# Attention scores and maxima as 64-row products, with one head of a pair in each half of the rows

## The chip, the core and the metric

The kernel runs on one core of a Trainium2 chip. The core has a matrix engine (TensorE, PE in the rows; its loads of the stationary operand are PEld), VectorE (DVE), ScalarE (ACT), GpSimd (POOL) and SyncE (SP), which here only issues DMAs. Products are written to PSUM, which has 8 banks of 128 partitions by 512 fp32 values. The metric is the device time of one launch in microseconds (us); the time before is the median of three runs.

## What is computed

Two layers of a diffusion backbone over 2048 latent tokens behind 256 context tokens, width 1024. Layer 0 is multi-head latent attention, layer 1 is gated linear attention. Only layer 0's attention is touched. Cut to that:

```python
q = concat(q_nope, axial_rope(q_rope))       # 16 heads, 64 + 32 columns each
k = concat(k_nope, broadcast(axial_rope(kr)))  # kr: 32 columns, the same for all heads
s = einsum('qhd,khd->hqk', q, k) * 96 ** -0.5  # latents read all 2304 tokens, context its own 256
o = einsum('hqk,khe->qhe', softmax(s), v)
y = (o * silu(gate)) @ w_out
```

The kernel computes `exp(s - max)` with the row maximum inside the product, and divides by the sum at the end. Each fp32 operand of a score product is split into a rounded high part and the rest (h and l, both of type F32R), and a score is the sum of three products, kh·qh + kh·ql + kl·qh. Maxima come from kh·qh alone.

## The kernel before

After the projections, attention runs over 8 pairs of heads, and in each pair over 5 chunks of queries: one of 256 context tokens and four of 512. One pair and chunk is a step (40 in all). A step goes over its keys in tiles of 128: 2 for the context chunk, 18 for the others. Step and key tile together are an item, 592 in all, of which 576 are 512 queries wide and 16 are 256 wide.

For one item `scores` (L578) makes a tile `st` of two PSUM banks, one bank for each head `j`, with three products a head (L592 to L594). The stationary operand is 128 keys, the moving one 512 queries, and the contraction is over 96 rows (64 of the head's own, 32 of the rotary part). The first product has a 97th row: ones in the key tile, and minus the row maximum in the query tile. ScalarE then takes the exponential of both banks (L596), and VectorE or GpSimd adds it to a running sum (L601, L603). `values` (L608) follows two items behind, for three key tiles at a time: it multiplies with v (L616), one head in the left 64 columns of the array and one in the right 64, in plain fp32. `finish` (L621) sums over partitions (L628) and normalises.

`maxima` (L460) runs ahead of the scores as a generator. For each step it makes, for a head, 128 queries and up to 512 keys, one product of 96 rows (L475) into a tile `pmx` and a VectorE maximum over it (L476): 40 of them in a full step, of which 8 are 256 wide, and 4 in a context step, 1312 in all. The pool of `pmx` has 3 banks; `st` has 4 and `po` 1. When a step's maxima are there they are transposed (L481), negated (L483) and sent by DMA into row 96 of the query tile (L485). The generator is stepped by a counter: in the query projections (`feed`, L511) up to a lead of 72, then 41 times a full step, spread evenly over the items (L690 to L708).

Keys are in four tiles `kb{b}{s}`, for even and odd pairs, high and low. `key_rows` (L413) puts the shared rotary rows into each of them, for both heads; `load_k` (L421) and `load_q` (L435) load a chunk by DMA, and GpSimd makes its high and low parts (L48, L53 by the helper `K`). All DMAs of these loads are issued by SyncE in the order of the program. The rest of the order of instructions on an engine is made by a scheduler when the program is built, from the order of the source, the dependences and the pools' buffers; so two engines' instructions may stand in another order than the source has them.

Of the kernel before, what the change touches and what calls it, by code (L numbers as in the profile page):

```python
# [19 lines left out]
P = 128  # L20
# [97 lines left out]
def body(ctx, tc, I, out, stop=99, dbg=None):  # L118
# [39 lines left out]
    qr_d = [dram.tile([2, 2, P, n], F32, name=f"qr{c0}_d") for c0, n in CHUNKS]  # L158
# [252 lines left out]
    kb = [[kvp.tile([97, 2, T], F32R, name=f"kb{b}{s}") for s in "hl"] for b in range(2)]  # L411

    def key_rows(b):  # L413
        for s in range(2):
            tc.keep_in_program_order(nc.sync.dma_start(kb[b][s][64:96, :, :].bitcast(F32), kr_d[s].unsqueeze(1).to_broadcast([32, 2, T])))
        tc.keep_in_program_order(nc.sync.dma_start(kb[b][0][96:97, :, :].rearrange("p j t -> p (j t)").bitcast(F32), onesr.bitcast(F32)))
# [4 lines left out]
    def load_k(pr, ci):  # L421

        c0, n = CHUNKS[ci]
        qf = qsp.tile([96, 2, 512], F32, name="kf", tag="qf", bufs=2)
        nc.sync.dma_start(qf[0:64, :, :n], k_d[ci][pr].rearrange("(h d) t -> d h t", h=2))

        def put():
            dst = [kb[pr % 2][s][0:64, :, c0:c0 + n] for s in range(2)]
            i_ = k.hi("p", dst[0], qf[0:64, :, :n])
            if pr == 0 and ci < 2:  # L430
                tc.keep_in_program_order(i_)
            k.lo("p", dst[1], qf[0:64, :, :n], dst[0])
        return put

    def load_q(si):  # L435
        pr, ci = steps[si]
        c0, n = CHUNKS[ci]
        qf = qsp.tile([96, 2, 512], F32, name="qf", tag="qf", bufs=2)
        nc.sync.dma_start(qf[0:64, :, :n], qn_d[ci][pr].rearrange("(h d) t -> d h t", h=2))
        for r in range(2):  # L440
            nc.sync.dma_start(qf[64 + 16 * r:80 + 16 * r, :, :n], qr_d[ci][pr // 4, r, 32 * (pr % 4):32 * (pr % 4) + 32, :].rearrange("(h d) t -> d h t", h=2))

        def put():
            qs = qsp.tile([97, 2, 2, 512], F32R, name="qs", tag="qs")
            k.hi("p", qs[0:96, 0, :, :n], qf[:, :, :n])
            k.lo("p", qs[0:96, 1, :, :n], qf[:, :, :n], qs[0:96, 0, :, :n])
# [13 lines left out]
    def maxima():  # L460

        for si, (pr, ci) in enumerate(steps):
# [7 lines left out]
            for j in range(2):  # L470
                for t in range(nq):
                    for b in range(npart):
                        w = min(512, keys - b * 512)
                        ps = pmp.tile([P, 512], F32, name="pmx")
# [1000 lines left out]
```

## Time and profile before

| | us |
|---|---|
| median of three runs (3830.13 to 3837.49) | 3831.97 |
| the profiled execution, its own time | 3830.01 |
| its span, first to last instruction | 3828.1 |
| the attention stage in it, first score product to last | 671.6 to 2450 |
| VectorE busy in 672 to 2450 | 1277.1 |
| mean granted TensorE clock, share of full speed | 0.985 |

A matmul's duration in the rows is longer than the distance to the next one, because products are pipelined and the profile models their ends. So what a product costs in a stream is read here from the starts of the rows, not from their durations. The rows read "start, duration" and merge neighbours of one kind; the count stands behind the x. An fp32 product (L616) is recorded as two matmuls, an F32R product (L475, L594) as one. A few matmul records can be missing.

### The profile page before, as it was taken

The numbers are of one execution on the slowest core, as the hardware profiler recorded it, in microseconds if no ns is written. First come the engines' busy times: TensorE is split into PE (matmuls) and PEld (weight loads), VectorE is DVE, ScalarE is ACT, GpSimd is POOL, SyncE is SP. The second block draws the span as 40 slices with busy tenths as digits, with TensorE's granted clock in tenths as the row PEclk, the third lists the DMA queues.
The fourth block names the chain that finished last, engine by engine and source line by source line (L and its number), as shares of the span: only waits on it lengthen the run. The fifth ranks groups of instructions, "written<-read, shape, count | busy, mean of one in ns | idle before, by whom it ended". The sixth has DMA issues, their size and how long they took to land.

```text
span 3828.1 us, 51918 instructions
## 1 busy us (share of the span) xinstructions
PE 3702.5 (97%) x20446; PEld 2717.6 (71%) x20446; DVE 2406.3 (63%) x3300; ACT 1356.5 (35%) x1991; POOL 1194.7 (31%) x731
## 2 busy tenths in 40 slices
PE   7999999999999999999999999999999999999799
PEld 5777887655555555555555655687999898999677
DVE  4332436777677777777777776465255677776863
ACT  2332221333333333333333333332224444443431
POOL 3121124646354363634546343455000101000000
PEclk8999999999999999999999999999999999999899
DMA  6120564302120121201101010276775666669332
GB/s 226 67 82 38 182 213 159 91 19 73 43 63 23 37 73 38 65 24 53 32 19 51 17 39 12 67 247 210 264 253 173 223 220 212 229 199 319 135 133 98
DMA packets 277245, 451.43 MB, mean 118 GB/s; under 512 B 21877, under 2 KB 178101, under 8 KB 264969
## 3 DMA queue, kind: packets, MB, share of 16 engines
q1 hardware_dynamic: 212504, 371.09, 29.5%
q10 hardware_dynamic: 64496, 77.02, 5.8%
q8 instruction: 161, 2.64, 0.3%
q14 instruction: 84, 0.68, 0.1%
HBM read 307.14 MB, written 140.71 MB: 117 GB/s over the span
## 4 chain that ended last, share of the span: by engine, by line
PE 76%; DMA 7%; DVE 6%; issue 6%; POOL 3%; ACT 2%; SPq 1%; POOLq 0%; ACTq 0%; DVEq 0%
PE st L594 20%; PE po L616 14%; PE pmx L475 8%; PE pj L61 5%; PE pj L60 5%; PE pj L62 5%; PE pp L893 2%; PE pp L894 2%; PE pp L895 2%; DMA wsg<-in_gla_w_in 2%; PE py L893 1%; PE py L895 1%; PE py L894 1%; PE pk L1060 1%; PE py L62 1%
## 5 line engine op out<-in xcount | busy, mean ns | idle before, releaser
L476 DVE TENSOR_REDUCE mx<-pmx 128x1 f32<-128x512 f32 (+1 forms) x1312 | 762.4, 624 | 320.5 <-PE pmx L475 319.8
L596 ACT ACTIVATE pe<-st 128x1024 f32<-128x1024 f32 (+1 forms) x592 | 599.3, 1013 | 1006.1 <-PE st L594 980.1
L603 POOL TENSOR_TENSOR acc<-acc,pe 128x1024 f32<-128x1024 f32 x192 | 468.5, 2440 | 571.1 <-ACT pe L596 570.4
L616 PE MATMUL po<-pe,vt 128*64 128x512 f32 (+1 forms) x2368 | 571.6, 598 | 0.0
L603 DVE TENSOR_TENSOR acc<-acc,pe 128x1024 f32<-128x1024 f32 x256 | 438.7, 1714 | 97.0 <-ACT pe L596 97.0
L594 PE MATMUL st<-qs,kb0h 97*128 97x512 f32 (+3 forms) x1184 | 375.7, 397 | 0.1
L594 PE MATMUL st<-qs,kb1h 97*128 97x512 f32 (+3 forms) x1184 | 374.9, 397 | 0.0
L616 PEld LDWEIGHTS po<-pe,vt 128*64 128x64 f32 x2368 | 156.7, 137 | 300.5 <-issue 297.1
L893 PE MATMUL pp<-w,ht 128*128 128x256 f32 x1088 | 317.9, 292 | 0.0
L894 PE MATMUL pp<-w,ht 128*128 128x256 f32 x1088 | 305.9, 281 | 0.0
L895 PE MATMUL pp<-w,ht 128*128 128x256 f32 x1088 | 304.9, 280 | 0.0
L594 PEld LDWEIGHTS st<-qs,kb1h 97*128 97x128 f32 (+1 forms) x1184 | 218.5, 190 | 57.4 <-issue 12.2
L594 PEld LDWEIGHTS st<-qs,kb0h 97*128 97x128 f32 (+1 forms) x1184 | 219.9, 190 | 49.1 <-issue 4.2
L594 PE MATMUL st<-qs,kb0l 96*128 96x512 f32 (+1 forms) x592 | 232.4, 393 | 0.0
L594 PE MATMUL st<-qs,kb1l 96*128 96x512 f32 (+1 forms) x592 | 232.1, 392 | 0.0
L1242 POOL TENSOR_TENSOR orr<-oss,mhalf 128x4 f32<-128x4 f32 x16 | 17.1, 1068 | 659.3 <-DVE oss L1241 659.3
L475 PE MATMUL pmx<-kb0h,qs 96*128 96x512 f32 (+1 forms) x656 | 209.0, 397 | 9.0 <-DVE mx L476 5.6
L475 PE MATMUL pmx<-kb1h,qs 96*128 96x512 f32 (+1 forms) x656 | 205.0, 396 | 4.1 <-DVE mx L476 4.0
L893 PEld LDWEIGHTS pp<-w,ht 128*128 128x128 f32 x1088 | 205.8, 189 | 3.4
L894 PEld LDWEIGHTS pp<-w,ht 128*128 128x128 f32 x1088 | 205.9, 189 | 1.1
L895 PEld LDWEIGHTS pp<-w,ht 128*128 128x128 f32 x1088 | 205.5, 189 | 0.1
L475 PEld LDWEIGHTS pmx<-kb1h,qs 96*128 96x128 f32 x656 | 114.0, 189 | 120.9 <-issue 73.7
(398 smaller groups left out, 7311.4 us busy)
## 6 DMA issues: line engine op xcount, KB each, us to landing
ht<-hh_d SPq DMA_DIRECT2D x44, 1024.0 KB
ht<-hl_d SPq DMA_DIRECT2D x44, 1024.0 KB
xt<-in_x SPq DMA_DIRECT2D x32, 512.0 KB
mod_w<-in_ada_w SPq DMA_DIRECT2D x16, 1024.0 KB
v<-gv_d SPq DMA_DIRECT2D x32, 512.0 KB
wsg<-in_gla_w_in SPq DMA_DIRECT2D x66, 192.0 KB
v_d<-vs ACTq DMA_DIRECT2D x18, 512.0 KB
vt<-v_d SPq DMA_DIRECT2D x8, 1152.0 KB
```

The source lines that it names most:

```text
L60: nc.tensor.matmul(ps, ah, bh, start=(i == 0), stop=False)
L61: nc.tensor.matmul(ps, ah, bl, start=False, stop=False)
L62: nc.tensor.matmul(ps, al, bh, start=False, stop=(i == n - 1))
L475: nc.tensor.matmul(ps[:, :w], qs[0:96, 0, j, t * P:t * P + P], kh[0:96, j, b * 512:b * 512 + w], start=True, stop=True)
L476: nc.vector.reduce_max(mx[:, j * nq + t, b:b + 1], ps[:, :w], axis=AX.X)
L594: nc.tensor.matmul(st[:, j, :n], a, b, start=(i == 0), stop=(i == 2))
L596: nc.scalar.activation(pe[:, :, :n], st[:, :, :n], AF.Exp, scale=SCALE)
L603: eng.tensor_tensor(acc[:, :, :n], acc[:, :, :n], pe[:, :, :n], op=ALU.add)
L616: nc.tensor.matmul(po[64 * j:64 * j + 64, :n], vt[:, kt, 64 * j:64 * j + 64], pe[:, j, :n], start=(kt == 0), stop=(kt == nk - 1))
L893: nc.tensor.matmul(ps, ah, bh, start=(i == 0), stop=False)
L894: nc.tensor.matmul(ps, ah, bl, start=False, stop=False)
L895: nc.tensor.matmul(ps, al, bh, start=False, stop=(i == n - 1))
```

## The change

The two heads of a pair are laid in the two halves of the 128 rows: head 0 in rows 0 to 63, head 1 in rows 64 to 127. Keys are now two tiles, `kbs0` and `kbs1` (even and odd pairs), each with a high and a low part of `T` = 2304 columns; `kbs1` also holds two tiles `kr` for all pairs. In each half `kr[0]` has the 32 rotary rows' high part and below it their low part; `kr[1]` has the high part and below it a row of ones. The query tile has the head's own 64 rows in one plane, and in a second plane the 32 rotary rows twice. The low plane's second copy gives its first row to minus the maximum.

A score is five products a head of 64 rows (the last of 33): kh·qh, kh·ql, kl·qh, `kr[0]` with the high rotary rows (both its parts at once), `kr[1]` with the low ones and the maximum. A maximum is two: kh·qh and `kr[0]` with the high rotary rows. The source writes them alternating between the heads, so that neighbours lie in different halves of the rows and in different banks. A unit of `maxima` is now one pair of tiles, both heads; its counters are halved (lead 36, 21 units a full step), and the number of tiles is the same.

```diff
+    kbs = [kvp.tile([P, 8 * D], F32R, name="kbs0"), kvp.tile([P, 4 * T], F32R, name="kbs1")]
+    kb = [[kbs[b][:, s * T:s * T + T] for s in range(2)] for b in range(2)]
+    kr = [kbs[1][:, s * T:s * T + T] for s in (2, 3)]
+    def key_rows():
+        for j in range(2):
+            for i, r0, s in ((0, 0, 0), (0, 32, 1), (1, 0, 0)):
+                tc.keep_in_program_order(nc.sync.dma_start(kr[i][64 * j + r0:64 * j + r0 + 32, :].bitcast(F32), kr_d[s]))
+            tc.keep_in_program_order(nc.sync.dma_start(kr[1][64 * j + 32:64 * j + 33, :].bitcast(F32), onesr[:, 0:T // P].bitcast(F32)))
...
-        for r in range(2):
-            nc.sync.dma_start(qf[64 + 16 * r:80 + 16 * r, :, :n], qr_d[ci][pr // 4, r, 32 * (pr % 4):32 * (pr % 4) + 32, :].rearrange("(h d) t -> d h t", h=2))
+        nc.sync.dma_start(qf[:, 0, :n], qn_d[ci][pr])
+        for j in range(2):
+            for u in range(2):
+                nc.sync.dma_start(qf[64 * j + 32 * u:64 * j + 32 * u + 32, 1, :n], qr_d[ci][pr, j])
...
-                        ps = pmp.tile([P, 512], F32, name="pmx")
-                        nc.tensor.matmul(ps[:, :w], qs[0:96, 0, j, t * P:t * P + P], kh[0:96, j, b * 512:b * 512 + w], start=True, stop=True)
-                        nc.vector.reduce_max(mx[:, j * nq + t, b:b + 1], ps[:, :w], axis=AX.X)
-                        yield
+                    ps = [pmp.tile([P, 512], F32, name="pmx") for _ in range(2)]
+                    for i, kk in enumerate((kh, kr[0])):
+                        for j in range(2):
+                            js = slice(64 * j, 64 * j + 64)
+                            nc.tensor.matmul(ps[j][:, :w], qs[js, 0, i, t * P:t * P + P], kk[js, bs], start=(i == 0), stop=(i == 1))
+                    for j in range(2):
+                        nc.vector.reduce_max(mx[:, j * nq + t, b:b + 1], ps[j][:, :w], axis=AX.X)
+                    yield
...
-    fed, lead, due = 0, 72, 0.0
+    fed, lead, due = 0, 36, 0.0
...
-            for j in range(2):
-                k3 = [(kh[0:97, j, ks], qs[0:97, 0, j, :n]), (kh[0:96, j, ks], qs[0:96, 1, j, :n]), (kl[0:96, j, ks], qs[0:96, 0, j, :n])]
-                for i, (a, b) in enumerate(k3):
-                    nc.tensor.matmul(st[:, j, :n], a, b, start=(i == 0), stop=(i == 2))
+            terms = [(kh, 0, 0, 64), (kh, 1, 0, 64), (kl, 0, 0, 64), (kr[0], 0, 1, 64), (kr[1], 1, 1, 33)]
+            for i, (a, s, r, m) in enumerate(terms):
+                for j in range(2):
+                    js = slice(64 * j, 64 * j + m)
+                    nc.tensor.matmul(st[:, j, :n], a[js, ks], qs[js, s, r, :n], start=(i == 0), stop=(i == len(terms) - 1))
...
-        total = sum(41 if ci else 5 for _, ci in steps)
+        total = sum(21 if ci else 3 for _, ci in steps)
```

Left out: the DRAM layout of the rotary queries, the chunk loads of the keys (one tile of 128 rows where it was 64 rows by two heads), and the output weights, which take over the same two key tiles.

On TensorE, in the sixth pair's third chunk of 512, from one group of value products to the next, the order before is this (`st` is a score tile, `pmx` a tile for maxima, `po` the output):

```order
L616 MATMUL po<-pe,vt 64x512 x6
L475 MATMUL pmx<-kb0h,qs 128x512 x3
L594 MATMUL st<-qs,kb1h 128x512 x2
L594 MATMUL st<-qs,kb1l 128x512
L594 MATMUL st<-qs,kb1h 128x512 x2
L594 MATMUL st<-qs,kb1l 128x512
L475 MATMUL pmx<-kb0h,qs 128x512
L475 MATMUL pmx<-kb0h,qs 128x256
L594 MATMUL st<-qs,kb1h 128x512 x2
L594 MATMUL st<-qs,kb1l 128x512
L594 MATMUL st<-qs,kb1h 128x512 x2
L594 MATMUL st<-qs,kb1l 128x512
```

Between two score groups of six products there stand two or three products for maxima, each in a bank of its own.

At the same place on TensorE the changed program has these rows (`kbs_3830` is the tile of even pairs, `kbs_3831` that of odd pairs and of the rotary rows):

```order
L625 MATMUL po<-pe,vt 64x512 x6
L484 MATMUL pmx<-kbs_3830,qs 128x256 x2
L484 MATMUL pmx<-kbs_3831,qs 128x256 x2
L603 MATMUL st<-qs,kbs_3831 128x512 x10
L484 MATMUL pmx<-kbs_3830,qs 128x512 x2
L484 MATMUL pmx<-kbs_3831,qs 128x512 x2
L603 MATMUL st<-qs,kbs_3831 128x512 x10
L484 MATMUL pmx<-kbs_3830,qs 128x512 x2
L484 MATMUL pmx<-kbs_3831,qs 128x512 x2
L484 MATMUL pmx<-kbs_3830,qs 128x512
L484 MATMUL pmx<-kbs_3831,qs 128x512
L603 MATMUL st<-qs,kbs_3831 128x512
```

A row of x2 is one product of each head, and the rows of x10 alternate between the heads. In the last four rows two units of maxima follow each other and the scheduler has taken the second apart: first both products of head 0, then one score product, then (not shown) both products of head 1 and the other nine of the scores.

On VectorE, from the same step, before (`mx` is a maximum over 256 or 512 keys, `acc` an addition to the running sum):

```order
L476 TENSOR_REDUCE mx<-pmx 128x1 x2
L603 TENSOR_TENSOR acc_13826<-acc_13826,pe 128x1024
L476 TENSOR_REDUCE mx<-pmx 128x1 x7
L603 TENSOR_TENSOR acc_13826<-acc_13826,pe 128x1024
L476 TENSOR_REDUCE mx<-pmx 128x1 x5
```

And VectorE in the changed program:

```order
L486 TENSOR_REDUCE mx<-pmx 128x1 x5
L612 TENSOR_TENSOR acc_16490<-acc_16490,pe 128x1024
L486 TENSOR_REDUCE mx<-pmx 128x1 x7
L612 TENSOR_TENSOR acc_16490<-acc_16490,pe 128x1024
L486 TENSOR_REDUCE mx<-pmx 128x1 x2
```

VectorE's work is the same in kind and number; additions stand between two and seven maxima, as before.

## Rows read from the trace of the kernel before

**Rows 1.** The page's busy time, share of the span and instructions; then its 40 slices.

```profile
PE 3702.5 (97%) x20446; PEld 2717.6 (71%) x20446; DVE 2406.3 (63%) x3300; ACT 1356.5 (35%) x1991; POOL 1194.7 (31%) x731
...
PE   7999999999999999999999999999999999999799
...
DVE  4332436777677777777777776465255677776863
```

**Rows 2.** The page's chain that ended last, shares of the span by line.

```profile
PE st L594 20%; PE po L616 14%; PE pmx L475 8%; PE pj L61 5%; PE pj L60 5%; PE pj L62 5%; PE pp L893 2%; PE pp L894 2%; PE pp L895 2%; DMA wsg<-in_gla_w_in 2%; PE py L893 1%; PE py L895 1%; PE py L894 1%; PE pk L1060 1%; PE py L62 1%
```

**Rows 3.** Busy time by stretch: us, then engines with counts, clock, DMA share, GB/s.

```profile
592.00:672.00 80.00, 78.61 (x333) 62.83 (x334) 54.84 (x98) 9.97 (x17) 27.48 (x22) 0.96 0.44 142
672.00:2450.00 1778.00, 1761.22 (x7513) 1038.42 (x7512) 1277.12 (x1705) 676.51 (x728) 853.92 (x407) 0.99 0.14 41
```

**Rows 4.** PE in order of time around 1500 us: start, duration, line, tiles, count.

```profile
1492.55 1.92 PE L72 MATMUL pmx<-mod_w,condT 128*32 128x512 f32 x16
...
1495.69 0.40 PE L594 MATMUL st<-qs,kb1l 96*128 96x512 f32 x1
1496.02 1.07 PE L616 MATMUL po<-pe,vt 128*64 128x512 f32 x2
...
1500.72 0.96 PE L475 MATMUL pmx<-kb0h,qs 96*128 96x512 f32 x3
1501.52 0.63 PE L594 MATMUL st<-qs,kb1h 97*128 97x512 f32 x2
...
1502.92 0.51 PE L475 MATMUL pmx<-kb0h,qs 96*128 96x512 f32 x2
```

**Rows 5.** The same around 2020 us, where a 256-wide step begins.

```profile
2020.83 0.40 PE L594 MATMUL st<-qs,kb0h 97*128 97x256 f32 x2
...
2021.54 0.28 PE L475 MATMUL pmx<-kb0h,qs 96*128 96x256 f32 x1
...
2022.81 2.79 PE L616 MATMUL po<-pe,vt 128*64 128x512 f32 x12
2025.63 0.50 PE L475 MATMUL pmx<-kb0h,qs 96*128 96x512 f32 x1
```

**Rows 6.** Weight loads (PEld) in order of time around 1498 us.

```profile
1497.02 0.97 PEld L82 LDWEIGHTS pmx<-sel,mod_s 128*128 128x128 f32 x8 [0.81 <-DVE mod_s L79]
1498.00 0.20 PEld L616 LDWEIGHTS po<-pe,vt 128*64 128x64 f32 x4
1498.48 0.14 PEld L616 LDWEIGHTS po<-pe,vt 128*64 128x64 f32 x2 [0.28 <-issue]
1498.91 0.14 PEld L616 LDWEIGHTS po<-pe,vt 128*64 128x64 f32 x2 [0.29 <-issue]
```

**Rows 7.** Weight loads waiting, 592 to 2450 us: total us, times, longest.

```profile
PEld pmx L475 <- DVE mx L476: 34.2, 48, 1.6
...
PEld pmx L475 <- DVE acc L603: 13.8, 17, 0.8
PEld pmx L475 <- DVE acc L606: 11.4, 14, 0.8
```

**Rows 8.** PE, DVE and POOL by line and shape, 592 to 2450 us: count, busy us, mean ns.

```profile
L475 PE MATMUL pmx<-kb0h,qs 96*128 96x512 f32 x512 | 186.0, 422 | 5.3 <-DVE mx L476 5.1
L476 DVE TENSOR_REDUCE mx<-pmx 128x1 f32<-128x512 f32 x1024 | 667.6, 683 | 254.9 <-PE pmx L475 254.7
L603 DVE TENSOR_TENSOR acc<-acc,pe 128x1024 f32<-128x1024 f32 x255 | 437.5, 1716 | 97.0 <-ACT pe L596 97.0
L53 POOL TENSOR_TENSOR qs<-qf,qs 96x1024 fp32r<-96x1024 f32 x32 | 81.4, 2542 | 2.5
L53 POOL TENSOR_TENSOR kb1l<-kf,kb1h 64x1024 fp32r<-64x1024 f32 x16 | 40.5, 2534 | 1.3
```

**Rows 9.** SP's DMA issues in order of time, 537 to 587 us: start, duration, tiles.

```profile
536.57 0.49 SPq L415 DMA_DIRECT2D kb0h<-krh_d  x1
...
587.05 1.05 SPq L441 DMA_DIRECT2D qf<-qr_d  x2
```

**Rows 10.** The view of rows 7 again: the only wait for a query tile.

```profile
PEld pmx L475 <- POOL qs L48: 3.4, 1, 3.4
```

More of the change, by code (lines that the diff above doesn't have):

```diff
@@ L157, in body @@
     qn_d = [dram.tile([NPAIR, P, n], F32, name=f"qn{c0}_d") for c0, n in CHUNKS]
-    qr_d = [dram.tile([2, 2, P, n], F32, name=f"qr{c0}_d") for c0, n in CHUNKS]
+    qr_d = [dram.tile([NPAIR, 2, 32, n], F32, name=f"qr{c0}_d") for c0, n in CHUNKS]
     v_d = dram.tile([T, D], F32, name="v_d")
@@ L423, in load_k @@
         c0, n = CHUNKS[ci]
-        qf = qsp.tile([96, 2, 512], F32, name="kf", tag="qf", bufs=2)
-        nc.sync.dma_start(qf[0:64, :, :n], k_d[ci][pr].rearrange("(h d) t -> d h t", h=2))
+        kf = qsp.tile([P, 2, 512], F32, name="kf", tag="qf", bufs=2)
+        nc.sync.dma_start(kf[:, 0, :n], k_d[ci][pr])
         def put():
-            dst = [kb[pr % 2][s][0:64, :, c0:c0 + n] for s in range(2)]
-            i_ = k.hi("p", dst[0], qf[0:64, :, :n])
+            dst = [kb[pr % 2][s][:, c0:c0 + n] for s in range(2)]
+            i_ = k.hi("p", dst[0], kf[:, 0, :n])
             if pr == 0 and ci < 2:
                 tc.keep_in_program_order(i_)
-            k.lo("p", dst[1], qf[0:64, :, :n], dst[0])
+            k.lo("p", dst[1], kf[:, 0, :n], dst[0])
         return put
@@ L469, in maxima @@
             npart = -(-keys // 512)
[L470 to L477 removed]
+            for t in range(nq):
+                for b in range(npart):
+                    w = min(512, keys - b * 512)
+                    bs = slice(b * 512, b * 512 + w)
+                    ps = [pmp.tile([P, 512], F32, name="pmx") for _ in range(2)]
[6 more added lines that the diff above has]
+                    yield
             mc = qsp.tile([P, 8], F32, name="mc", bufs=2)
@@ L529, in body @@
                     fetch()
-                if ci == 4 and pr == 5:
-                    key_rows(1)
                 ps = psp.tile([P, 512], F32, name="pj")
@@ L679, in out_weights @@
         def out_weights(b, raw):
-            w2 = [kvp.tile([P, 4, D], F32R, name=f"wo{b}{s}", tag=f"kb{b}{s}") for s in "hl"]
+            w = kvp.tile([P, 8 * D], F32R, name=f"wo{b}", tag=f"kbs{b}")
+            w2 = [w[:, 4 * D * s:4 * D * s + 4 * D].rearrange("p (k n) -> p k n", k=4) for s in range(2)]
             for kt in range(4):
@@ L705, in body @@
                     fetch(1)
-                while fed < min(lead, fed0 + 0.2 * i) + rate * (i + 1):
+                while fed < min(lead, fed0 + 0.1 * i) + rate * (i + 1):
                     fed += 1
```

23 lines of the change are left out of this document (8 added, 15 removed).

## The prediction

> **What bounds the kernel now.** I read the page's busy shares first, then the chain that ended last, then the attention stage alone, then starts of single products in it. TensorE is busy for 97% of the span and at 9 tenths in nearly every slice, VectorE at 7 in the slices of attention [rows 1]. The chain runs through TensorE, and three of its largest shares are the lines of attention: scores 20%, value products 14%, maxima 8% [rows 2]. In 672 to 2450 us TensorE is busy for 1761 of 1778 us at a granted clock of 0.99 (the 2.4 GHz level), VectorE for 1277 us, or 72% [rows 3]. So this stage is bound by how many product slots TensorE needs, with VectorE near enough to cause waits.
>
> What a slot costs comes from the starts. From 1501.52 to 1502.92 us six score products follow each other [rows 4]: 1.40 / 6 = 0.233 us for 512 columns. From 2020.83 to 2021.54 us six products of 256 columns take 0.71 [rows 5]: 0.118 us. The durations of 0.4 us in those rows overlap and are not used.
>
> **Score and maxima products.** Removed: 592 items x 6 score products (3456 of 512 columns, 96 of 256) and 1312 maxima products (1024 and 288). That is 4480 x 0.233 + 384 x 0.118 = 1089 us of slots. Added: ten products an item and two a maximum, of 64 rows. If two neighbours in different row halves share a slot, ideal pairing would need 2880 + 1024 = 3904 slots of 512 and 80 + 288 = 368 of 256: 953 us, a gain of 136. All of it comes from the scores (5 slots for 6). The maxima, two products of half the rows, gain nothing.
>
> The order that the program was built with doesn't pair ideally. I counted neighbours in it: 4033 pairs of opposite halves, and 478 products that stand beside one of their own half. The latter come at 83 places where two units of maxima follow each other and the second is taken apart, because the pool has 3 banks for two pairs of tiles (the last rows of the changed TensorE order show one). By width: 4126 slots of 512 and 385 of 256, 4126 x 0.233 + 385 x 0.118 = 1007 us. So the slots give **-82 us**.
>
> **Do two halves share a slot?** No product of before uses part of the rows, so this is bounded from both sides. The nearest row is the value products, which use halves of the columns: 12 recorded products from 2022.81 to 2025.63 us [rows 5], 2.82 us. Their loads come two at a time, 0.43 us apart [rows 6], so six pairs fill 6 x 0.43 = 2.6 us and the rest is entry and exit; one after another, 12 would take 5.2. Column halves do share. I take the same for row halves, as the nearest row; the other end is no sharing at all (a rival below). For the slot itself I keep 0.233; the value products' 0.43 for two passes over 512 columns would be 0.214, the low end.
>
> **Weight loads.** A pair of slots now needs two loads of 128 columns. Eight such loads in a row take 0.97 us, the last of them 0.19 [rows 6]: (0.97 - 0.19) / 7 = 0.111 us apart. Even if the two queue on one path, 0.222 fits under 0.233. It doesn't fit under 0.118: 227 pairs of maxima and 71 of scores are 256 wide, 298 x 0.104 = 31 us. The column halves' loads run two at a time [rows 6], so I take 0 and keep 31 for the range.
>
> **Changes of the array's shape.** Last full-array score product to first column-half product: 1495.69 to 1496.02 us, 0.33 instead of 0.233 [rows 4]. On the way back, three maxima products take 1500.72 to 1501.52 = 0.80 us instead of 0.70 [rows 4]. So a change costs 0.10 us on leaving and 0.10 on entering. Before, the value products already force them. The built order has 862 changes before and 941 after; the 79 new ones are mostly maxima between full-array products in the query projections. 79 x 0.2 = **+16 us**, on the path, since TensorE is busy there too (78.6 of 80 us) [rows 3].
>
> **Waits for VectorE.** VectorE's instructions are the same in number and size. Before, maxima products waited for it 48 + 17 + 14 = 79 times, for 34.2 + 13.8 + 11.4 = 59 us [rows 7], 0.75 us each. What is queued behind the waiting product is all of TensorE: the next scores, and through them ScalarE. VectorE ends each maximum when it did, but TensorE arrives one slot earlier per item, so each wait grows by about one slot: 79 x 0.233 = **+18 us**. That the waits vanish (-59) or grow much (a rival) is kept for the range.
>
> **Edits at nothing.** GpSimd splits a key chunk as 128 x 512 instead of 64 x 1024, half the elements per row; the query tile stays at 1024 a row [rows 8]. GpSimd is at 48% in the stage [rows 3]; the gain of slack is worth nothing. Rotary queries take four DMAs instead of two, 80 more issues of about 0.52 us [rows 9] on SyncE; behind them stand the DMAs of the next loads and of the maxima's row. Both are used over a step later, and the only recorded wait for a query tile is one of 3.4 us [rows 10]. If that cover went, each step would lose the two issues, 1 us. The shared key rows are loaded once, by eight DMAs at the start instead of three then and three later, each one of them smaller; the stage they feed could start later by the issues, 5 x 0.5 = 2.5 us [rows 9]. The lead of the maxima is the same in tiles.
>
> **Sum.** -82 + 16 + 18 = -48 us. Against the profiled execution's own 3830.0 that is 3782; the median of the runs shown is 2.0 above it, so **3784 us**.
>
> **The rivals.**
>
> *VectorE takes the gain (the one that ends slower).* A pair of maxima holds two of three banks. At the 83 places where a second pair follows, its second tile waits for the first pair's first maximum. If an addition stands ahead of that on VectorE, the maximum ends 0.42 + 1.72 + 0.68 = 2.82 us after the pair's last product starts [rows 8], while TensorE has only a slot, two single products and one score product to do, 4 x 0.233 = 0.93. That is 1.89 us x 83 = 157 us of waits against 59 before: -82 + 16 + 98 = +32, 3864 us. It decides from a mean wait of (59 + 66) / 83 = 1.5 us on. For it: VectorE's 72% become 74, and its additions still stand anywhere among the maxima in the built order. Against: the mean before is 0.75, with three banks too.
>
> *The halves' loads are exposed.* Then a slot is 0.233 + 0.111: 4511 x 0.111 = 501 us more, -82 + 16 + 18 + 501 = +453, 4285 us. Against it: a pair of column halves passes 512 columns twice in 0.43 us, less than two F32R slots (0.466), so none of its loads of 0.14 us is in that time [rows 4 to 6]. The Trainium skill has the rule behind this rival, in "TensorE: Matmul & The Clock Gate", section "Part 3: Packing small matmuls — row/col tiling": a load overlaps a running matmul only where their row groups differ. By it each half's load would wait for its own half's product, at the price just given; the value products' rows, whose halves have all rows in common, disagree with it.
>
> *The halves don't run together.* Then the change doesn't do what it says: 5760 + 2048 products of 512 and 160 + 576 of 256, 1906 us for 1089: +817, 4649 us with nothing else. For it: no row shows row halves, and these are F32R products where the column halves are fp32. Against: columns share, in quarters too (sixteen products of 32 columns in 1.92 us [rows 4], 0.12 each).
>
> *A faster one.* A pair's slot is 0.214: 4126 x 0.019 = 78 us less, 3706 us.
>
> **How the numbers follow.** The forecast, halves sharing a slot and waits a little longer, has 60% and its own range is 3735 to 3824 (slot 0.225 with fewer waits; 31 us of loads and some 10 us of longer waits). The faster rival has 12% (3700 to 3735). VectorE taking the gain has 17%, of which 6% fall within 0.2% of before and 11% above. Exposed loads 5%, no sharing 6%. 0.2% is 7.7 us, about what a measurement of this kernel can tell from no change. So faster 72%, same 6%, slower 22%. The range 3700 to 3865 leaves out the two slow rivals (11%), and some 3% at each end.
>
> **What would show it.** In the profile after: the two heads' score products starting a few ns apart and pairs about 0.233 us apart (an item's ten in 1.17 us); value products unchanged at 2.82 us for twelve; waits for `mx` and `acc` at maxima products near 80 us in total; the stage shorter by about 60 us and the projections before it longer by some 10. I am wrong about sharing if the ten take 2.3 us, about loads if pairs are 0.34 apart, and about VectorE if the waits come to 130 us or more.

## The result and the profile after

The changed kernel takes 3942.07 us (median of four runs, 3936.72 to 3945.12), the kernel before beside it 3834.73: a ratio of 1.0274, 95% interval 1.0248 to 1.0300. Slower, where 3784 us and "faster" were forecast, and outside the range of 3700 to 3865. The profiled execution takes 3936.72 us, 106.7 more than the profiled one of before.

The page's busy line, as in [rows 1]:

```profile
PE 3716.6 (94%) x24126; PEld 2674.0 (68%) x24126; DVE 2404.2 (61%) x3300; ACT 1357.8 (35%) x1991; POOL 1133.0 (29%) x731
```

TensorE is busy for 94% of a longer span, before for 97%. The two stretches of [rows 3], with their new limits (columns as there):

```profile
595.00:693.00 98.00, 96.75 (x400) 62.41 (x400) 56.59 (x98) 9.98 (x17) 34.75 (x30) 0.96 0.40 119
693.00:2557.00 1864.00, 1757.32 (x11130) 996.07 (x11132) 1275.16 (x1706) 677.58 (x728) 788.84 (x399) 0.97 0.13 41
```

From the starts of the products: the first maxima product comes 3.4 us later, at 595.54 us (the only wait for a query tile stands ahead of it); from it to the first score product at 693.16 pass 97.6 us instead of 79.4 (+18.2); from there to the last score product at 2556.60, the stage, 1863.4 instead of 1778.7 (+84.7); the tail is the same to 0.3 us. VectorE does the same work (1275 us for 1277). The granted clock of the attention stage fell from 0.99 to 0.97.

Do two row halves share a slot? TensorE in order of time, as [rows 4, 5]:

```profile
1503.15 0.86 PE L484 MATMUL pmx<-kbs,qs 64*128 64x512 f32 x4
1503.62 1.56 PE L603 MATMUL st<-qs,kbs 64*128 64x512 f32 x10
1504.79 0.85 PE L484 MATMUL pmx<-kbs,qs 64*128 64x512 f32 x4
1505.25 1.54 PE L603 MATMUL st<-qs,kbs 64*128 64x512 f32 x10
1506.72 2.79 PE L625 MATMUL po<-pe,vt 128*64 128x512 f32 x12
1509.45 0.74 PE L484 MATMUL pmx<-kbs,qs 64*128 64x512 f32 x4
```

From 1503.15 to 1504.79 us, four maxima and ten score products, 14 products in 7 pairs, take 1.64 us: 0.234 a pair. So they share, with two loads a slot hidden (256-wide pairs too: of two maxima pairs behind scores, the second starts 0.12 us after the first), and the value products are as before (2.79 us for twelve). What was gained there went elsewhere. Waits of TensorE's weight loads (total us, times, longest), the rows that answer to [rows 7, 10]; then TensorE's own waits, in which a load that waits behind a running product doesn't count:

```profile
PEld pmx L484 <- DVE mx L486: 191.2, 260, 4.0
...
PEld pmx L491 <- DVE mc L489: 21.7, 22, 3.4
PEld pmx L491 <- ACT pe L605: 21.5, 15, 1.4
...
PEld pmx L484 <- DVE acc L612: 19.5, 24, 0.8
...
PEld pmx L484 <- POOL qs L48: 8.8, 1, 8.8
```

```profile
PE pmx L484 <- DVE mx L486: 66.1, 67, 3.8
PE pmx L491 <- ACT pe L605: 15.3, 15, 1.0
PE pmx L491 <- DVE mc L489: 13.7, 16, 2.9
```

and the same two groups of TensorE's own waits in the kernel before:

```profile
PE pmx L475 <- DVE mx L476: 9.6, 12, 1.2
PE pmx L481 <- DVE mc L479: 3.6, 5, 2.6
```

Loads for maxima products now wait 284 times for 211 us, before 79 times for 59; TensorE itself stands still for 66 us over that, before 10. The transposes of the maxima (L491) add 29, before 3.6. Where it stands longest is the end of a step. All engines there, in order of time (start, duration, idle time before and its releaser in brackets):

```profile
1529.14 1.23 DVE L612 TENSOR_TENSOR acc<-acc,pe 128x1024 f32<-128x1024 f32 x1
1529.21 3.39 POOL L53 TENSOR_TENSOR qs<-qf,qs 128x1024 fp32r<-128x1024 f32 x1
...
1530.29 0.68 DVE L486 TENSOR_REDUCE mx<-pmx 128x1 f32<-128x512 f32 x1
1530.89 2.79 DVE L615 TENSOR_TENSOR acc<-acc,acc 128x1024 f32<-128x1024 f32 x1
...
1533.61 2.68 DVE L486 TENSOR_REDUCE mx<-pmx 128x1 f32<-128x512 f32 x4
...
1534.34 0.79 PE L484 MATMUL pmx<-kbs,qs 64*128 64x512 f32 x1 [2.12 <-DVE mx L486]
...
1534.94 2.32 PE L603 MATMUL st<-qs,kbs 64*128 64x512 f32 x6
1537.19 4.44 PE L625 MATMUL po<-pe,vt 128*64 128x512 f32 x12
```

VectorE is on the step's last addition, `acc0 += acc1` (L615), for 2.79 us, while GpSimd makes the low part of a later step's query tile (L53); the maximum that frees a bank is queued behind it, and TensorE waits 2.12 us for that. The twelve value products behind it take 4.44 us instead of 2.79. The clock by stretches (columns as in [rows 3], the clock is the third value from the end):

```profile
1515.00:1533.00 18.00, 16.20 (x105) 9.99 (x101) 14.54 (x17) 5.63 (x6) 9.48 (x5) 1.00 0.01 1
1533.00:1541.00 8.00, 6.66 (x19) 2.98 (x21) 3.17 (x5) 1.02 (x1) 0.00 (x0) 0.57 0.21 66
1541.00:1555.00 14.00, 12.97 (x90) 7.06 (x88) 7.19 (x15) 6.25 (x8) 4.16 (x3) 1.00 0.13 39
```

0.57 between 1533 and 1541 us: the lower level, 1.2 GHz, for nearly all of it; TensorE had stood for 0.93 us ahead of 1531.03, and was standing for the 2.12 when the clock fell. In the stage the trace has 21 such falls, before five, and 113 us at the lower level, before 24. Of TensorE's 18 waits over 1.5 us there, 16 have a fall in them or right behind them. Over the whole span the mean clock is 0.973 for 0.985; each 0.01 is 0.02 of the span at 1.2 GHz, so 2 x 0.027 x 3935 = 212 us against 2 x 0.015 x 3828 = 115: 97 us more at half speed, an estimate of some 49 us. The same addition in both kernels, its duration's least, median and greatest in ns, after and then before:

```profile
L615 DVE TENSOR_TENSOR acc<-acc,acc x32: 1207/2784/2800, 754.7 to 2560.4; 128x1024 f32<-128x1024 f32 x32
```

```profile
L606 DVE TENSOR_TENSOR acc<-acc,acc x32: 1206/1209/6380, 732.6 to 2455.0; 128x1024 f32<-128x1024 f32 x32
```

In the changed kernel 19 of the 32 last additions start while GpSimd's split runs; each ends 1.08 us after the split does. Before, 21 of the 32 splits meet an earlier addition, which ends 1.08 us after it too, but each time TensorE goes to its value products meanwhile and doesn't wait. Around 1521.54 us:

```profile
1521.29 2.39 POOL L53 TENSOR_TENSOR qs<-qf,qs 96x1024 fp32r<-96x1024 f32 x1
...
1521.54 3.22 DVE L603 TENSOR_TENSOR acc<-acc,pe 128x1024 f32<-128x1024 f32 x1
...
1523.86 2.80 PE L616 MATMUL po<-pe,vt 128*64 128x512 f32 x12
...
1524.69 0.68 DVE L476 TENSOR_REDUCE mx<-pmx 128x1 f32<-128x512 f32 x1
1525.29 1.21 DVE L606 TENSOR_TENSOR acc<-acc,acc 128x1024 f32<-128x1024 f32 x1
```

Where the stage's 84.7 us went can be estimated from the starts of its products in both traces: 0.233 us for a slot of 512 columns, 0.429 for a pair of value products, up to 0.10 at a change of shape, twice as long at 1.2 GHz; what is left ahead of a product is its delay. Slots and changes then give -75 us, the slower clock +40, delays of maxima products +90 (129 for 39) and of the transposes +30 (35 for 5); the rest cancels. With 0.230 or 0.236 for a slot the first term moves by up to 6 us, the clock and the delays by 1.

### The profile page after: what moved, and what is told of

Same layout as the page of the kernel before. It is cut to its first block, busy times and chain, and to the rows that moved or that the text cites. A ratio compares the mean times of both kernels' runs of the same rounds, so it can differ in the third digit from the quotient of the medians.

```text
span 3934.7 us, 59342 instructions
## 1 busy us (share of the span) xinstructions
PE 3716.6 (94%) x24126; PEld 2674.0 (68%) x24126; DVE 2404.2 (61%) x3300; ACT 1357.8 (35%) x1991; POOL 1133.0 (29%) x731
## 4 chain that ended last, share of the span: by engine, by line
PE 68%; issue 8%; DVE 8%; DMA 7%; POOL 4%; ACT 3%; SPq 1%; ACTq 0%; POOLq 0%; DVEq 0%
PE st L603 15%; PE po L625 14%; PE pmx L484 7%; PE pp L903 3%; PE pj L61 3%; PE pj L60 3%; PE pj L62 3%; PE pp L905 3%; PE pp L904 3%; DVE mx L486 2%; DMA wsg<-in_gla_w_in 2%; ACT pe L605 1%; PE pg L1141 1%; PE py L903 1%; DVE acc L612 1%
## 5 line engine op out<-in xcount | busy, mean ns | idle before, releaser
L603 PE MATMUL st<-qs,kbs 64*128 64x512 f32 (+2 forms) x5920 | 913.3, 396 | 0.7 <-DVE t L562 0.6
L603 PEld LDWEIGHTS st<-qs,kbs 64*128 64x128 f32 (+1 forms) x5920 | 630.3, 187 | 130.6 <-issue 20.7
L484 PE MATMUL pmx<-kbs,qs 64*128 64x512 f32 (+1 forms) x2624 | 514.4, 400 | 79.0 <-DVE mx L486 66.1
L625 PE MATMUL po<-pe,vt 128*64 128x512 f32 (+1 forms) x2368 | 584.8, 623 | 1.4 <-DMA vt<-v_d 1.4
L484 PEld LDWEIGHTS pmx<-kbs,qs 64*128 64x128 f32 x2624 | 277.9, 187 | 366.1 <-DVE mx L486 191.2
L612 DVE TENSOR_TENSOR acc<-acc,pe 128x1024 f32<-128x1024 f32 x256 | 405.7, 1585 | 141.1 <-ACT pe L605 134.5
L903 PE MATMUL pp<-ht,w 128*128 128x256 f32 (+1 forms) x616 | 184.3, 300 | 10.1 <-ACT vge L968 6.0
L904 PE MATMUL pp<-ht,w 128*128 128x256 f32 (+1 forms) x616 | 176.4, 286 | 0.0
L905 PE MATMUL pp<-ht,w 128*128 128x256 f32 (+1 forms) x616 | 175.6, 285 | 0.1
L1127 ACT ACTIVATE ex<-df 128x512 f32<-128x512 f32 x192 | 114.2, 632 | 148.3 <-DVE df L1124 132.0
L114 POOL TENSOR_TENSOR rs_r<-rs_v,mhalf 128x1 f32<-128x1 f32 x52 | 29.3, 564 | 379.6 <-DVE rs_v L112 378.1
```

The costliest lines, as they stand in the source:

```text
L484: nc.tensor.matmul(ps[j][:, :w], qs[js, 0, i, t * P:t * P + P], kk[js, bs], start=(i == 0), stop=(i == 1))
L603: nc.tensor.matmul(st[:, j, :n], a[js, ks], qs[js, s, r, :n], start=(i == 0), stop=(i == len(terms) - 1))
L612: eng.tensor_tensor(acc[:, :, :n], acc[:, :, :n], pe[:, :, :n], op=ALU.add)
L625: nc.tensor.matmul(po[64 * j:64 * j + 64, :n], vt[:, kt, 64 * j:64 * j + 64], pe[:, j, :n], start=(kt == 0), stop=(kt == nk - 1))
L903: nc.tensor.matmul(ps, ah, bh, start=(i == 0), stop=False)
L904: nc.tensor.matmul(ps, ah, bl, start=False, stop=False)
```

## The experiments

Each is compared with runs of the kernel before on the same chip; ratios are to these, with their 95% interval. Ratios of kernels that leave work out tell only where time goes.

**Is it VectorE's work?** Three kernels of the changed one make VectorE's part smaller, a fourth does so in the kernel before.

```diff
# after_short_max, before_short_max, after_neither (ps[:, :64] in before)
-                        nc.vector.reduce_max(mx[...], ps[j][:, :w], axis=AX.X)
+                        nc.vector.reduce_max(mx[...], ps[j][:, :64], axis=AX.X)
# after_no_adds, after_neither
-            elif len(seen) > 1:
+            elif len(seen) > 1 and e == 1:
# all four, so that nothing overflows
-            nc.scalar.activation(pe[...], st[...], AF.Exp, scale=SCALE)
+            nc.scalar.activation(pe[...], st[...], AF.Exp, scale=SCALE * 0.001)
```

> The changed kernel with each maximum taken over the first 64 columns of its tile, so VectorE needs a fraction of the time for it (the exponent is scaled down so that nothing overflows; the output is not the reference's). If VectorE's waits at the maxima products are what cost the 107 us, they vanish, and the tiles are no longer taken apart in the built order (976 us of slots instead of 1007): about 3740 to 3780 us. If the row halves themselves cost more on TensorE than counted (changes of the array's shape, loads, longer slots), the time stays above 3860 us.

Measured 3858.3 us, 1.0067 (1.0040 to 1.0094): a miss, 78 us above the range's end and 2 us short of the rival's range.

> The same cut in the kernel before: maxima over the first 64 columns of a tile, exponent scaled down. It had 59 us of waits for VectorE: about 3775 to 3800 us. With the run above it gives what the change is worth on TensorE alone: if the banks theory holds, the changed kernel is faster by 20 to 60 us here; if the row halves cost more than counted, it is slower here too.

Measured 3811.0 us, 0.9956 (0.9929 to 0.9983).

> The changed kernel without VectorE's running additions from the third key tile on (GpSimd's stay; the sums and the output are wrong, the exponent is scaled down). The built order of the products is the same, taken apart at the same places. If maxima wait because an addition of 1.6 us stands ahead of them on VectorE, nearly all waits go: 3830 us or less. If the waits come from two pairs of tiles sharing three banks whatever else VectorE does, most stay: 3890 us or more.

Measured 3841.0 us, 1.0027 (1.0012 to 1.0041), between the two theories.

> The changed kernel with both of VectorE's loads cut: maxima over the first 64 columns of a tile, and no running additions from the third key tile on (the output is wrong; exponent scaled down). What is left is TensorE's own time. If VectorE's maxima and additions together explain the loss, the waits at maxima products fall under 30 us and the time to 3740 to 3775 us. If something on TensorE itself (changes of shape, loads) costs more than counted, it stays above 3800 us.

Measured 3794.4 us, 0.9916 (0.9896 to 0.9936), again between. With hardly any work on VectorE the change wins 32 us on the kernel before as it is. But shorter maxima alone bring before 19 us down, so more than half of that isn't the change's. The waits that are left in this run (loads, 590 to 2424 us):

```profile
PEld pmx L484 <- DVE mx L486: 58.4, 101, 2.2
PEld pmx L491 <- issue: 42.3, 29, 4.1
```

So most of the new waits need VectorE's work, maxima and additions both. And one thing was told only later: the last addition of a step, which all these kernels keep, took 1.23 us in after_no_adds and 2.52 in after_short_max (means), and the stage's clock was 0.98 and 0.97. In before_short_max it took 2.57, with the clock at 0.99: long additions alone don't cost the time.

**Is it the order of the units?** after_place lets at most one unit stand ahead of an item's scores, and puts the extra one just ahead of the value products; 964 us of slots by its built order instead of 1007 (972 in the expectation).

```diff
-                while fed < min(lead, fed0 + 0.1 * i) + rate * (i + 1):
+                goal = min(lead, fed0 + 0.1 * i) + rate * (i + 1)
+                if fed < goal:
                     fed += 1
                     next(stream, None)
...
+                while fed < min(goal, total):
+                    fed += 1
+                    next(stream, None)
                 for si, kt, nk in items[nv:i - 1]:
                     values(si, kt, nk)
```

> The changed kernel with a second unit of maxima never in front of the same item's scores but just ahead of the value products, where VectorE then has 2.8 us for it. The built order takes 10 places apart instead of 83 (972 us of slots instead of 1007). If the waits at the places taken apart and their single slots are the larger part of the loss, 3835 to 3865 us. If most waits come at ordinary places because VectorE is the bound of the stage, above 3905 us.

Measured 3856.0 us, 1.0068 (1.0042 to 1.0094), as expected: it lies 26 us above the kernel before beside it, the changed kernel 107, so some 81 us of the loss are the taken-apart units and where they stand. By the same estimate from the starts, 48 of them are slots, 28 shorter delays of maxima and transposes, 5 the clock. But TensorE still waits 64.9 us for maxima (66.1 in the changed kernel). before_pairs gives the kernel before the changed one's grain, units of two tiles with halved counters, and nothing else.

```diff
-            for j in range(2):
-                for t in range(nq):
-                    for b in range(npart):
-                        ps = pmp.tile([P, 512], F32, name="pmx")
...
+            for t in range(nq):
+                for b in range(npart):
+                    ps = [pmp.tile([P, 512], F32, name="pmx") for _ in range(2)]
...
-    fed, lead, due = 0, 72, 0.0
+    fed, lead, due = 0, 36, 0.0
```

> The kernel before, products of 96 rows, with nothing changed but the unit of the maxima: two tiles, one of each head, taken together from the three banks, counters halved as in the changed kernel. If taking two of three banks at a time is enough to make the waits, it is slower than before by 25 to 80 us (3855 to 3910). If the waits need the faster scores and two tiles that end at the same moment, it is within 10 us of before.

Measured 3871.7 us, 1.0114 (1.0098 to 1.0130), as expected: the grain alone costs some 45 us, with full-array products and no more VectorE work.

**Less or shorter additions on VectorE**, both on after_place: two more key tiles added by GpSimd, and each addition as two of 512.

```diff
-            e = 1 if kt % 2 == 1 and 2 < nk and kt < nk - 2 else 0
+            e = 1 if (kt % 2 == 1 or kt in (4, 10)) and 2 < nk and kt < nk - 2 else 0   # after_place_pool
...
+                for u in range(2 if e == 0 else 1):                                       # after_place_halves
+                    us = slice(u, u + 1) if e == 0 else slice(0, 2)
+                    eng.tensor_tensor(acc[:, us, :n], acc[:, us, :n], pe[:, us, :n], op=ALU.add)
```

> As after_place, with two of the ten key tiles of a step that VectorE adds up given to GpSimd (key tiles 4 and 10). If additions ahead of maxima make a good part of the waits left in after_place (about 200 us), they fall by a fifth or more: 3805 to 3835 us. If only the banks count, 3850 us or more; slower than that if GpSimd's longer additions slow VectorE's.

Measured 3859.9 us, 1.0085 (1.0070 to 1.0100): a miss, nothing gained; the rival's range.

> As after_place, with each of VectorE's running additions as two of 512 columns, so that no maximum stands behind more than 0.8 us of one addition, if the built order puts maxima between the two. VectorE does the same adding with some 0.06 us more for each. If the length of one addition matters: 3815 to 3840 us. If VectorE's total work matters: 3856 us or more.

Measured 3878.3 us, 1.0144 (1.0123 to 1.0166): a miss, worse; the rival's range. Neither edit helped. That doesn't show that the amount of additions is nothing, since after_no_adds wins some 96 us on the changed kernel: after_place_pool leaves the step's last addition where it was, and TensorE has the same 19 waits over 1.5 us behind it as in after_place, 48 us. In after_place_halves they stand behind another addition (below).

**Does a unit wait because it takes two of three banks at once?** after_skew shifts the heads: head 0's two products beside head 1's first two score products, head 1's beside head 0's last two. The tiles of a full unit are then taken five slots apart.

```diff
+            mine = [(score, i) for i in range(len(terms))]
+            row = [[(f, i) for f in units for i in range(2)] + mine, mine + [(f, i) for f in units for i in range(2)]]
+            for i in range(len(row[0])):
+                for j in range(2):
+                    row[j][i][0](j, row[j][i][1])
```

> The changed kernel, with each full unit of maxima shifted against the scores: head 0's two products stand beside the first two score products of head 1, head 1's two beside the last two score products of head 0, so every pair of neighbours still lies in opposite halves, but the unit's two tiles are taken and given back one after another, five slots apart, not both at once. Units of 256 keys stay pairs of tiles. By the built order the slots are 974 us (1007 in the changed kernel, 964 in after_place). Theory that a unit waits because it needs two of three banks at once: the waits of maxima products for VectorE fall from after_place's 180 us to 60 to 110, and the time from 3856 to 3750 to 3800 us, below the kernel before. Rival, that VectorE's order of additions and maxima alone makes the waits, whatever TensorE's order: waits of 150 us or more and 3840 to 3880 us.

Measured 3929.1 us, 1.0252 (1.0223 to 1.0281): a miss by over 120 us, and the theory that I held by then fell. Pairing still works, but the waits stand as before, and longer. TensorE and VectorE at a step's end of after_skew:

```profile
1523.80 0.79 PE L486 MATMUL pmx<-kbs,qs 64*128 64x512 f32 x1 [3.31 <-DVE mx L488]
```

```profile
1518.63 1.22 DVE L632 TENSOR_TENSOR acc<-acc,pe 128x1024 f32<-128x1024 f32 x1
1519.95 3.19 DVE L635 TENSOR_TENSOR acc<-acc,acc 128x1024 f32<-128x1024 f32 x1
```

The last addition again, now 3.19 us, but in 7 of the 32 steps only. Of TensorE's waits over 1.5 us for a maximum, 6 stand behind it and 14 behind an earlier addition that meets GpSimd's split. The stage's clock was 0.95.

**Do additions stand at the head of VectorE's queue, waiting for ScalarE?** after_place_lag and before_lag issue each addition two items later (`late.append((e, pe))`, taken out when more than two are in it or the step ends).

> after_place with each addition to the running sums issued two items later, so that its exponential is long there when VectorE comes to it; same work. Theory that additions waiting for ScalarE at the head of VectorE's queue hold the maxima up: waits of maxima products for VectorE fall from 180 us to 140 or less, 3800 to 3835 us. Rival, that only the banks matter: 3845 to 3870 us with waits near 180.

Measured 3858.0 us, 1.0074 (1.0052 to 1.0097): the bank theory's range, though that theory fell with after_skew; loads still waited 160.8 us for maxima, and the 19 waits behind the last addition are those of after_place.

> The kernel before with the same lag of two items for the additions, as the control of after_place_lag. Its maxima wait for only 59 us in all, so at most some 20 us can go: 3805 to 3835 us by either theory.

Measured 3823.7 us, 0.9980 (0.9967 to 0.9994).

**Does TensorE outrun VectorE between two groups of value products?** The groups come after two key tiles instead of three (after_even2 on after_place, before_even2 on before).

```diff
-            if i >= 2 and (items[i - 2][1] % 3 == 2 or items[i - 2][1] == items[i - 2][2] - 1):
+            if i >= 2 and items[i - 2][1] % 2 == 1:
```

> after_place with the value products after every two key tiles instead of three; same work, 168 more changes of the array's shape (17 to 34 us). Theory of the local rate: between two groups of value products VectorE has more to do (3.3 pairs of maxima of 0.65 us each tile and 1.3 additions of 1.7 us, 6.6 us) than TensorE now takes for three items (some 5 us), and three banks don't carry it over; with shorter stretches of scores the waits of maxima products for VectorE fall from 199 us to 100 or less, and the time to 3770 to 3830 us. Rival, that additions at the head of VectorE's queue hold the maxima up wherever the values stand: waits of 170 us or more, 3865 to 3890 us.

Measured 3844.9 us, 1.0043 (1.0028 to 1.0058): neither theory's range, with 246 + 48 us of waiting loads instead of 100 or less. I take the theory as fallen.

> The kernel before with the value products after every two key tiles, as the control of after_even2. Its maxima wait for 59 us, so by the local rate at most 40 us can go against 17 to 34 us of changes of shape: 3810 to 3850 us. By the rival 3845 to 3865 us.

Measured 3903.7 us, 1.0191 (1.0174 to 1.0208): a miss, 54 us above its range and 39 above the rival's.

> after_even2 with each addition issued two items later, as in after_place_lag. If the shorter stretches make the waits short, what is left of them is additions that wait for ScalarE, and the lag takes some of it: 10 to 30 us below after_even2. By the theory of the local rate alone it changes nothing: within 8 us of after_even2.

Measured 3857.2 us, 1.0079 (1.0064 to 1.0094), 12 us above after_even2: a miss. In these kernels the last addition of a step took 2.73 us on average in after_even2 and 2.26 in before_even2, where it took 1.42 in before. The edit had moved that meeting too, so these three say little on what they were meant for. In before_even2 no long wait of TensorE stands behind that addition, and why that kernel loses 75 us stays open.

**The step's last addition.** That pointed at a row that most of the slow kernels share, but not all, and a fast one has it too (after_place_halves at 1.0144, then before_short_max at 0.9956):

```profile
L617 DVE TENSOR_TENSOR acc<-acc,acc x32: 1207/1208/1225, 752.9 to 2500.9; 128x1024 f32<-128x1024 f32 x32
```

```profile
L606 DVE TENSOR_TENSOR acc<-acc,acc x32: 1225/3198/3424, 729.2 to 2435.8; 128x1024 f32<-128x1024 f32 x32
```

What the slow ones share is wider: an addition, the last or an earlier one, that meets GpSimd's split while TensorE needs a maximum behind it. So stand TensorE's waits over 1.5 us for a maximum in the changed kernel (15 of 15, 13 behind the last addition), after_place (21 of 21, 19 behind the last), after_place_halves (20 of 21, none behind the last) and after_skew (20 of 21, 6 behind the last). The merge kernels take the last addition from VectorE: the products with ones sum over both running sums, four of them a step where two stood.

```diff
-            if kt == nk - 1 and st_["seen"][1]:
-                nc.vector.tensor_tensor(st_["acc"][0][:, :, :n], st_["acc"][0][:, :, :n], st_["acc"][1][:, :, :n], op=ALU.add)
...
-            for j in range(2):
-                nc.tensor.matmul(pss[64 * j:64 * j + 64, :n], ones[:, 0:64], acc[:, j, :n], start=True, stop=True)
+            accs = [a for a, s in zip(st_["acc"], st_["seen"]) if s]
+            for u, a in enumerate(accs):
+                for j in range(2):
+                    nc.tensor.matmul(pss[64 * j:64 * j + 64, :n], ones[:, 0:64], a[:, j, :n], start=(u == 0), stop=(u == len(accs) - 1))
```

> The changed kernel, with the step's last addition (acc0 += acc1) taken from VectorE: the products with ones sum over both running sums instead, 4 products where 2 stood, some 0.45 us of TensorE a step, +14 us. Theory that the long waits come from that addition, which the trace of after shows at 2.79 us (1.45 before) because GpSimd splits the next query tile at the same moment, and that the granted clock falls behind them: the 22 waits over 1.5 us (51 us) nearly go, the low clock in the stage falls from 112 us to 70 or less (20 us back): 3942 to 3860 to 3900 us. Rival, that VectorE is behind everywhere and the wait only moves to the next addition: waits still near 200 us, 3930 to 3960 us.

Measured 3880.5 us, 1.0131 (1.0109 to 1.0154), as expected: 50 us above the kernel before beside it instead of 107, so some 58 us back from one addition of 1.2 us a step, with the products that replace it paid. TensorE's own waits for maxima, and the stage with its clock:

```profile
PE pmx L484 <- DVE mx L486: 33.0, 54, 3.8
```

```profile
694.00:2505.00 1811.00, 1738.27 (x11250) 992.74 (x11252) 1224.81 (x1675) 677.54 (x728) 788.26 (x399) 0.99 0.14 43
```

33 us for 66, and the clock back at 0.99, with 44 us at the lower level in the stage for 113. By the estimate from the starts: delays of maxima -33, clock -30, added products +14.

> The same on top of after_place: by the theory its 24 waits over 1.5 us (63 us) and the clock behind them go, against 14 us of products: 3856 to 3785 to 3825 us, below the kernel before. By the rival 3850 to 3875 us.

Measured 3801.6 us, 0.9922 (0.9899 to 0.9946), as expected: **faster than both kernels**, 29 us or 0.8% below the 3830.7 of before beside it, with the interval clear of 1. TensorE's own waits for maxima:

```profile
PE pmx L484 <- DVE mx L486: 18.8, 33, 3.8
```

> The kernel before with the same edit, as the control: it has six waits of that kind (9 us), so it pays the products: 3825 to 3845 us by either theory.

Measured 3826.6 us, 0.9989 (0.9977 to 1.0002): no difference that can be told. So in the kernel before the addition cost no more than about the 14 us of products that replace it; the edit wins only where the heads share slots.

**Why does it take 2.79 us?** after_pieces leaves the addition in its place and cuts GpSimd's low part of the query tile into pieces of 128 columns.

```diff
-            k.lo("p", qs[:, 1, :, :n], qf[:, :, :n], qs[:, 0, :, :n])
+            for r in range(2):
+                for h in range(0, n, 128):
+                    k.lo("p", qs[:, 1, r, h:h + 128], qf[:, r, h:h + 128], qs[:, 0, r, h:h + 128])
```

> The changed kernel, with GpSimd's low part of the query tile made in pieces of 128 columns, eight instructions where one of 1024 stood; same work. Theory that VectorE's additions stand still for as long as the one GpSimd instruction that they meet runs (the step's last addition takes 1.21 us in 11 steps and 2.79 in 20, and in these it ends 1.1 us after GpSimd's): the additions that took 2.8 to 3.4 us take 1.7 or less, the 22 waits over 1.5 us are less than 8, the low clock falls from 112 us to 75 or less, 3942 to 3890 to 3915 us. Rival, that the two share their path in halves and the added time is the same however it is cut: additions still 2.4 us or more, 3930 us or more.

Measured 3924.0 us, 1.0237 (1.0210 to 1.0265): half a hit. The addition in this kernel:

```profile
L617 DVE TENSOR_TENSOR acc<-acc,acc x32: 1212/1292/1306, 755.0 to 2541.3; 128x1024 f32<-128x1024 f32 x32
```

So it isn't slowed, it is shut out while one GpSimd instruction runs, and short instructions let it in: 1.29 us for 2.78. That mechanism is shown. But the time fell by some 18 us, where 27 to 52 were expected. TensorE's own waits for maxima are 41.4 us, those at the transposes rose to 42 from 29, which took back 13, and the stage's clock stays at 0.97:

```profile
PE pmx L493 <- DVE mc L491: 26.9, 16, 4.4
PE pmx L493 <- ACT pe L607: 15.3, 15, 1.0
```

```profile
692.00:2538.00 1846.00, 1749.15 (x11131) 992.74 (x11132) 1240.35 (x1707) 678.23 (x728) 862.20 (x623) 0.97 0.14 42
```

The clock still falls 17 times in the stage, with 102 us at the lower level; to take the addition away was worth over three times as much as to shorten it. So the collision is only a part of what that addition costs at the step's end.

## Why the prediction was wrong, step by step

**The slots: right in kind.** Pairs come 0.234 us apart, as costed (0.233), and neither the exposed loads nor halves that run apart showed. The Trainium skill, "TensorE: Matmul & The Clock Gate", section "Part 3: Packing small matmuls — row/col tiling", has a load overlap a running product only where their row groups differ. These rows don't agree: neighbours of one half follow each other at the pair's distance, with loads of 187 ns hidden. No single run shows the -82 us by itself; the estimate from the starts gives -65 to -76 for the slots of the stage.

**Changes of the array's shape: right.** +16 forecast, 18.2 measured from the first maxima product to the first score product. There a pair of maxima starts 0.32 us after a full-array product, and a full-array product 0.33 after a pair, where before both distances were 0.23. The first maxima product, 3.4 us late, was costed at up to 2.5; the wait ahead of it is 8.8 us where it was 3.4.

**Waits for VectorE: the step that failed.** The text kept the number of waits at 79 and let each grow by one slot. Their mean stayed (211 / 284 = 0.74 us for 0.75); their number went to 284, and by the starts the maxima products of the stage are delayed by 90 us more, where +18 stood. To reason from the old waits one by one left out all the products that had not waited so far, with a slack below what the change took away. before_pairs shows that the grain alone, two tiles at once from three banks, costs 45 us. The prediction saw that VectorE's queue was as long as before, and took the same mean for a sign that nothing else would come of it.

**VectorE takes the gain: the right rival, too narrow.** It gave 17%, and 3864 us. It had the mechanism, an addition ahead of the maximum that frees a bank, but only at 83 taken-apart places, and with the mean addition of 1.72 us [rows 8]. The long waits stand at the step's end, behind an addition that GpSimd shuts out. Its bound of 130 us of waits was met: 211.

**The clock was in no term.** The 0.99 of [rows 3] was read as a fixed condition. Behind TensorE's waits it falls, and what was 0.985 over the span became 0.973, some 49 us of products. after_merge and after_skew show the coupling at both ends: 0.99 with 33.0 us of TensorE waiting for maxima, 0.95 with 83.1.

**"The gain of slack on GpSimd is worth nothing": wrong the other way.** GpSimd's busy time wasn't the question; when it runs was. Its split starts when a step's last score products release the query tile, and by the new timing it meets the step's last addition, in 19 of 32 steps, with TensorE short of a maximum. The trace of before had the meeting in plain sight (3.22 us for an addition beside GpSimd's split, 1.21 without) behind a mean of 1716 ns [rows 8], but with value products on TensorE. The Trainium skill says why, in "SBUF — State Buffer", section "SBUF: two separate sides": VectorE with two SBUF inputs and GpSimd share one pair of ports as an exclusive lock, and whoever starts first has it for the whole instruction. This trace agrees: the addition ends 1.08 us after GpSimd's instruction (1533.68 and 1532.60 us), and 1.21 alone.

**The sum again.** Against the forecast's -48 us stand, from the starts: slots and changes of the stage -75, maxima +90, transposes +30, clock +40, the stretch ahead of the stage +18, the later first product +3. That is +106 for +107. TensorE's own waits for maxima (66 us for 10) are only part of the 90. The rest are products that start late without an idle TensorE in the rows, most likely behind loads that waited: of the 211 us of waiting loads, 145 lie behind a running product, before 49 of 59.

**What stays open.** Why the transposes wait longer even in after_place_merge (29.4 us for the last maximum) was not tried; nor was GpSimd's split moved away from the step's end with the additions left as they are; nor were kernels with a fourth bank for the maxima, since scores, values and maxima have all eight.

## What to carry to other kernels

A gain on the busiest engine can be lost to the engine that feeds it, and the feeder's slack is to be counted over all places where it could run out, above all where a step ends and long instructions come together, not only over the waits that exist. Look at the spread of an instruction's time and not at its mean: a second value in it, here 2.79 beside 1.21 us, names a collision that the change may move: it costs nothing while TensorE has other products to do, and a stop where it needs what stands behind it. When a stall is on TensorE's path, cost what the clock does behind it too.

## What the hardware showed unexpectedly

- Two row halves of the array run F32R products of 64 rows at once, 0.234 us a pair of 512 columns, the second half's start typically 4 ns after the first, each with its own load hidden.
- A VectorE addition of two tensors of 1024 columns takes 1.21 us alone and up to 3.4 us when it meets GpSimd's split of a query tile, ending 1.08 us after it at the 19 and 21 places above; beside eight splits of 128 columns it takes 1.29.
- Around two stops of TensorE, 0.93 and 2.12 us, the granted clock fell to 0.57 from 1533 to 1541 us, and twelve value products took 4.44 us instead of 2.79. Sixteen such falls more in the 32 full steps make the 0.02 by which the stage's clock fell.
